# Closing branch A's softmax sums: reciprocals spread by TensorE transposes, or through DRAM by DMA

## The chip, the cores and the metric

The kernel runs on one core of one Trainium2 chip. The metric is the device time of one execution in microseconds. An execution is timed several times; a separate profiled execution leaves a trace, in which the span is the time from its first to its last instruction. The engines are TensorE (PE; its weight loads are PEld), VectorE (DVE), ScalarE (ACT), GpSimd (POOL) and SyncE (SP), which here issues most DMAs. Each engine works its own instruction list strictly from top to bottom, and an instruction that waits holds up all behind it.

## The reference

An encoder layer over two sequences, one of 1024 positions and one of 256 (together T = 1280, ten tiles of 128). Cut to what matters here:

```python
o_a, _ = _banded_attention(qa, ka, va, A_WINDOW, 1, rel_bias[:, :A_HEADS], sink)   # 8 heads of 64
    # inside: denom = sum(p) + exp(sink - m);  o = (p @ v) / denom
o_b = _dilated_mixture(qb, kb, vb, rel_bias[:, A_HEADS:])
merged = gates[:, :, 0] * (o_a.reshape(b, S, A_Q) @ w_branch_a) + gates[:, :, 1] * (o_b @ w_branch_b)
x = x + merged @ w_out
```

The gates are sigmoids of 2 x 1024 columns of the input projection plus a bias. After this come an RMS norm, a squared-ReLU MLP and a last RMS norm. All is float32; a product of two float32 matrices is made of three matmuls on parts that are split into a high and a low half (`hi`, `lo`): ScalarE writes the high half, VectorE subtracts it from the source to get the low half.

## The kernel before, in words

The kernel projects everything first, then runs branch B's attention, then branch A's (eight heads in four units of two, ten tiles of 128 queries each), then the gated merge, then the MLP. The change lies at the seam between branch A's attention and the gated merge, some 665 to 760 us into the span.

**Branch A's attention.** For each pair of tiles, scores are made, exponentiated (ScalarE, which also sums each row into `l_a`, a tile of 128 queries x 8 heads x 10 tiles), turned by TensorE, and multiplied with the values. The result leaves unnormalized to DRAM (`scr_o`, lines 1212 and 1213), already transposed: 128 rows are two heads' 64 channels, columns are queries. `sums_a` (line 1215) closes the sums: it adds the sink's term and takes the reciprocal, in the layout queries x (head, tile). In between TensorE works off `logits` (line 1223), the gates' last projections, whose PSUM blocks ScalarE copies out (`gs`, line 1234) for SyncE to store in DRAM (`scr_g`, line 1235).

**Reciprocals meet the output.** The output has channels on its partitions and the reciprocals have queries there. So `widen` (line 1394) lets GpSimd repeat each reciprocal 64 times (line 1398), and `turn_a` (line 1400) lets TensorE transpose that by four 128x128 transposes per tile into PSUM (line 1408) before VectorE multiplies (line 1409) the reloaded output `o` (`load_o`, line 1387). ScalarE then writes the high half (line 1415) and VectorE the low half (`low_a`, line 1419).

**The gated merge.** `jobs` lists the products: for each of three blocks of columns (512, 512, 256) eight products of branch B, then four of branch A; last, four more of branch A for each block. Below they are numbered from 0: jobs 0 to 7 are branch B's of the first block (six matmuls each), jobs 8 to 11 branch A's of the first block (twelve each). Each product fills one of three PSUM banks named `mm`, which go round: job 7 takes the bank of job 4, and so on. VectorE multiplies the bank with the job's gate (`mT`, line 1535, or `sg`, line 1537), which frees it. Job *i*'s gate is loaded by SyncE (`load_gate`, line 1481: `sg<-scr_g`, 256 KB) six jobs ahead, and ScalarE applies the sigmoid (`open_gate`, line 1486) three jobs ahead. Weights of branch A (`w_a`) are loaded by `fetch` (line 222), and split by `prepare` (lines 231 and 235, `whi` and `wlo`); `weight(0)` at a job calls for the next.

**What sets the order.** Up to `last.close()` the instructions of each engine stand as the code is written. From there, the jobs' loop included, a scheduler places each engine's instructions by its own costs, keeping the order of data. All DMAs named here are on SyncE's one queue. They use eight semaphores in turn, so a DMA also waits for the eighth before it to have landed.

## Time and profile before

| | |
|---|---|
| device time, median of 3 runs | 1674.3 us (1673.67 to 1675.32) |
| span of the profiled execution | 1672.7 us (its device time is not given apart; the median lies 1.6 us above this span) |
| TensorE busy | 1661.8 us (99%), granted clock 1.000 on the mean |
| VectorE, ScalarE, GpSimd busy | 951.1, 714.3, 494.3 us |
| TensorE idle from 655 to 800 us | 0.8 us, one wait, at 695.3 us |

In rows of the trace the number ahead is the start in us from the span's start, the next the duration; "128x512 f32" is partitions by elements of what is written; a bracket at the end holds the idle time of the engine before the row and what ended it. "SPq" rows are DMAs as SyncE issues them, not the transfer itself.

### The profile page before, as it was taken

Reading aid. Unit: us, or ns where it says so; the run is one execution under the profiler, and the core shown is the slowest. Engines: PE = TensorE matmul, PEld = TensorE weight load, DVE = VectorE, ACT = ScalarE, POOL = GpSimd, SP = SyncE. Lnnn points to the kernel's source line nnn. Section 1 sums busy time; section 2 is a strip of 40 time slices with the busy share of each in tenths; the row PEclk is TensorE's granted clock in tenths of the full one; section 3 lists DMA queues with packets and bytes.
Section 4 is the critical chain, followed back from the end, with each engine's and each line's share of the span. In section 5 each row is a group of like instructions: output and inputs, shape, how many; then the busy total and the mean of one; then the engine's idle time right before and its main releaser. Section 6 shows DMA issues by size and latency. Waiting matters only on the chain.

```text
span 1672.7 us, 24767 instructions
## 1 busy us (share of the span) xinstructions
PE 1661.8 (99%) x9256; PEld 1413.9 (85%) x9256; DVE 951.1 (57%) x1534; ACT 714.3 (43%) x1473; POOL 494.3 (30%) x372
## 2 busy tenths in 40 slices
PE   9999999999999999999999999999999999999998
PEld 7898888888888888888888888888888888888886
DVE  6732233455654565667278545445456775867665
ACT  6232323345654655654176333333334333333435
POOL 1212222111112352100100656455554250514240
PEclk9999999999999999999999999999999999999999
DMA  7416552666667794845121443343356934733333
GB/s 256 150 54 126 134 132 75 165 196 189 198 184 228 192 236 134 284 135 193 38 89 59 161 160 120 121 161 125 116 191 230 362 113 137 253 104 107 120 120 126
DMA packets 224176, 262.45 MB, mean 157 GB/s; under 512 B 29486, under 2 KB 153694, under 8 KB 224056
## 3 DMA queue, kind: packets, MB, share of 16 engines
q1 hardware_dynamic: 217000, 242.69, 45.4%
q0 software_dynamic: 6720, 17.65, 5.1%
q8 instruction: 73, 1.20, 0.3%
q10 hardware_dynamic: 336, 0.53, 0.1%
q14 instruction: 47, 0.39, 0.1%
HBM read 175.13 MB, written 90.92 MB: 159 GB/s over the span
## 4 chain that ended last, share of the span: by engine, by line
PE 96%; ACT 2%; DVE 1%; DMA 1%; issue 0%; SPq 0%; DVEq 0%; ACTq 0%
PE dn L345 22%; PE x L345 19%; PE mm L192 14%; PE z L345 10%; PE v L819 6%; PE y L345 5%; PE mm L345 5%; PE pv L345 3%; PE sc L345 3%; PE pt L1193 2%; PE pv L1209 2%; PE sc L553 1%; PE pv L600 1%; PE pt L586 1%; PE tr L336 1%; PE sc L1167 1%
## 5 line engine op out<-in xcount | busy, mean ns | idle before, releaser
L345 PE MATMUL dn<-dhi,ulo 128*128 128x512 f32 x448 | 174.3, 389 | 0.0
L345 PE MATMUL dn<-dlo,uhi 128*128 128x512 f32 x448 | 174.3, 389 | 0.0
L345 PE MATMUL dn<-dhi,uhi 128*128 128x512 f32 x448 | 174.3, 389 | 0.0
L345 PE MATMUL x<-chi,wlo 128*128 128x512 f32 x424 | 166.5, 393 | 0.0
L345 PE MATMUL x<-clo,whi 128*128 128x512 f32 x424 | 165.6, 390 | 0.0
L345 PE MATMUL x<-chi,whi 128*128 128x512 f32 x424 | 165.0, 389 | 0.0
L312 DVE TENSOR_TENSOR wlo<-ta,whi 128x1024 fp32r<-128x1024 f32 x30 | 56.3, 1876 | 174.0 <-ACT whi L310 174.0
L312 DVE TENSOR_TENSOR wlo<-raw,whi 128x1024 fp32r<-128x1024 f32 x60 | 89.6, 1494 | 103.1 <-ACT whi L310 98.2
L391 POOL TENSOR_TENSOR tb<-raw 128x512 f32<-128x512 f32 x25 | 32.3, 1290 | 363.7 <-DMA raw<-in_w_in_dram 111.8
L345 PEld LDWEIGHTS dn<-dhi,ulo 128*128 128x128 f32 x448 | 84.1, 188 | 17.6
L345 PEld LDWEIGHTS dn<-dhi,uhi 128*128 128x128 f32 x448 | 84.1, 188 | 17.4
L345 PEld LDWEIGHTS dn<-dlo,uhi 128*128 128x128 f32 x448 | 84.1, 188 | 17.4
L345 PEld LDWEIGHTS x<-chi,whi 128*128 128x128 f32 x424 | 79.6, 188 | 17.1
L345 PEld LDWEIGHTS x<-chi,wlo 128*128 128x128 f32 x424 | 79.8, 188 | 15.1
L345 PEld LDWEIGHTS x<-clo,whi 128*128 128x128 f32 x424 | 79.8, 188 | 14.6
L1735 POOL TENSOR_TENSOR t<-raw,t 128x1024 f32<-128x1024 f32 x16 | 46.4, 2924 | 149.2 <-DMA raw<-in_w_down_dram 149.2
L186 DVE TENSOR_TENSOR ulo<-uraw,uhi 128x1024 fp32r<-128x1024 f32 x56 | 86.1, 1558 | 4.4 <-ACT uhi L185 4.4
L1886 DVE TENSOR_TENSOR v<-v,dn 128x512 f32<-128x512 f32 x90 | 59.7, 683 | 42.3 <-PE dn L345 42.3
L186 DVE TENSOR_TENSOR dlo<-raw,dhi 128x1024 fp32r<-128x1024 f32 x32 | 50.1, 1590 | 46.3 <-ACT dhi L185 45.3
L1986 POOL TENSOR_TENSOR u<-u,u 128x640 f32<-128x640 f32 x16 | 25.1, 1569 | 173.3 <-ACT u L1904 173.3
L345 PE MATMUL dn<-dhi,up 128*128 128x512 f32 x224 | 73.5, 389 | 0.0
L345 PE MATMUL z<-chi,wlo 128*128 128x512 f32 x184 | 71.6, 389 | 0.0
(319 smaller groups left out, 4619.2 us busy)
## 6 DMA issues: line engine op xcount, KB each, us to landing
scr_u<-u SPq DMA_DIRECT2D x112, 320.0 KB, 2.6
uraw<-scr_u SPq DMA_DIRECT2D x56, 512.0 KB, 3.9
raw<-in_w_down_dram SPq DMA_DIRECT2D x36, 512.0 KB, 6.7
raw<-in_w_up_dram SPq DMA_DIRECT2D x32, 512.0 KB, 5.2
raw<-in_w_in_dram SPq DMA_DIRECT2D x25, 512.0 KB, 5.2
sg<-scr_g SPq DMA_DIRECT2D x32, 256.0 KB, 6.2
uraw<-scr_u SPq DMA_DIRECT2D x28, 256.0 KB, 4.5
qk<-scr_kb SPq DMA_DIRECT2D x48, 128.0 KB, 2.6
```

Source lines behind the costliest of these rows:

```text
L186: nc.vector.tensor_tensor(lo, src, hi.bitcast(F32), op=ALU.subtract)
L192: nc.tensor.matmul(ps, a, b, start=i == 0, stop=i == len(seq) - 1)
L312: nc.vector.tensor_tensor(lo, src, hi.bitcast(F32), op=ALU.subtract)
L336: nc.tensor.transpose(ps[:, P * i : P * (i + 1)], xn[t][:, P * k : P * (k + 1)], ident)
L345: nc.tensor.matmul(ps, a, b, start=first and i == 0, stop=last and i == len(seq) - 1, skip_group_check=True)
L391: (nc.vector if vector else nc.gpsimd).tensor_tensor(o, x, y, op=ALU.subtract)
L819: nc.tensor.matmul(ps[:, :n], a, b, start=k == 0 and j == 0, stop=k == KC - 1 and j == 2)
L1193: nc.tensor.transpose(ps[:, P * k : P * k + P], s[:, h, P * b : P * b + P], ident)
L1209: nc.tensor.matmul(pv[HALVES[h], P * i : P * i + P], src, pt[:, at + 2 * b + h, :], start=b == 0, stop=b == W // P - 1, skip_group_check=True)
L1735: nc.gpsimd.tensor_tensor(o, a, b, op=ALU.subtract)
L1886: nc.vector.tensor_tensor(v, v, ps, op=ALU.add)
L1986: nc.gpsimd.tensor_tensor(u[S1], u21, u22, op=ALU.add)
```

## The change

The repeat on GpSimd, the forty transposes and their PSUM banks go. `sums_a` runs earlier, in the last round of the attention loop, behind the last transposes of scores. A new `rows_a` transposes the reciprocals once (128 x 80 to 80 x 128), VectorE copies them out of PSUM, and SyncE stores these 80 rows (40 KB) in a DRAM buffer `scr_l1`. `widen` now is two DMAs on SyncE for each pair of tiles, each reading four rows' stretches of 256 floats once for each of 64 partitions (256 KB each); `turn_a` multiplies with that tile. Two weights of `w_a` are fetched and split at jobs one lower (0, 3, 4, 7 in place of 1, 4, 5, 8).

```diff
--- before.py
+++ after.py
@@ -277,6 +277,7 @@
     scr_n = dram.tile([2, ROWS * P], F32, name="scr_n")
     scr_c = dram.tile([1, ROWS * P], F32, name="scr_c")
     scr_o = [dram.tile([P, 4, 2, P], F32, name=f"scr_o{t}") for t in range(0, NT, 2)]
+    scr_l1 = dram.tile([AH, T], F32, name="scr_l1")
     scr_x = [dram.tile([P, D], F32, name=f"scr_x{t}") for t in range(NT)]
 
     scr_u = [dram.tile([P, 7, 4, TH], F32, name=f"scr_u{g}") for g in range(FF // P // 8)]
@@ -1212,14 +1213,6 @@
             nc.vector.tensor_copy(o, pv[:, : 2 * P].rearrange("p (i q) -> p i q", i=2))
             nc.sync.dma_start(scr_o[t // 2][:, u], o)
 
-        def sums_a():
-
-            sinks = nsink.unsqueeze(2).to_broadcast([P, AH, NT])
-            nc.vector.tensor_tensor(nm_a, nm_a, sinks, op=ALU.subtract)
-            nc.scalar.activation(nm_a, nm_a, AF.Exp)
-            nc.vector.tensor_tensor(l_a, l_a, nm_a, op=ALU.add)
-            nc.vector.reciprocal(l_a, l_a)
-
         def logits():
 
             for i, c in enumerate(PLAIN):
@@ -1389,24 +1382,12 @@
                 rows_o[t] = slot("o", (P, 4, 2, P))
                 nc.sync.dma_start(rows_o[t], scr_o[t // 2])
 
-        wide_l = {}
-
-        def widen(t):
-
-            r = wide_l[t // 2] = slot("wl", (P, 2, AH, HD))
-            for i in range(2):
-                nc.gpsimd.tensor_copy(r[:, i], l_a[:, :, t + i].unsqueeze(2).to_broadcast([P, AH, HD]))
-
         def turn_a(t):
             if t in (0, 4, 8):
                 o_hi.block(t // 4)
                 o_lo.block(t // 4)
             o = rows_o[t - t % 2][:, :, t % 2, :]
-            ps = bank("pt")
-            r = wide_l[t // 2][:, t % 2].rearrange("p h d -> p (h d)")
-            for k in range(4):
-                nc.tensor.transpose(ps[:, P * k : P * k + P], r[:, P * k : P * k + P], ident)
-            nc.vector.tensor_tensor(o, o, ps.rearrange("p (k q) -> p k q", k=4), op=ALU.mult)
+            nc.vector.tensor_tensor(o, o, wide_l[t // 2][:, :, P * (t % 2) : P * (t % 2) + P], op=ALU.mult)
             per = o_hi.per(P * t)
             parts = [(o_hi.at(k, P * t, P, per), o_lo.at(k, P * t, P, per), o[:, k : k + per, :])
                      for k in range(0, 4, per)]
@@ -1417,6 +1398,32 @@
         def low_a(t):
             for hi, lo, src in banks_t.pop(("a", t)):
                 nc.vector.tensor_tensor(lo, src, hi.bitcast(F32), op=ALU.subtract)
+
+        def sums_a():
+
+            sinks = nsink.unsqueeze(2).to_broadcast([P, AH, NT])
+            nc.vector.tensor_tensor(nm_a, nm_a, sinks, op=ALU.subtract)
+            nc.scalar.activation(nm_a, nm_a, AF.Exp)
+            nc.vector.tensor_tensor(l_a, l_a, nm_a, op=ALU.add)
+            nc.vector.reciprocal(l_a, l_a)
+
+        def rows_a():
+
+            ps, n = bank("mm", "tn"), AH * NT
+            nc.tensor.transpose(ps[:n, :P], l_a.rearrange("p h t -> p (h t)"), ident)
+            rows = a3("o", (P, 2, P), 3)[:n, 0, :]
+            nc.vector.tensor_copy(rows, ps[:n, :P])
+            a = scr_l1[:, :]
+            nc.sync.dma_start(bass.AP(a.tensor, a.offset, [[P, n], [1, P]]), rows)
+
+        wide_l = {}
+
+        def widen(t):
+
+            r = wide_l[t // 2] = slot("wl", (P, 4, 2 * P))
+            a = scr_l1[:, :]
+            for h in range(2):
+                nc.sync.dma_start(r[HALVES[h]], bass.AP(a.tensor, a.offset + T * h + P * t, [[0, HD], [2 * T, 4], [1, 2 * P]]))
 
         load_h21()
         load_prompt(0, unit0[0])
@@ -1444,6 +1451,7 @@
                 for h in range(2):
                     exponential(*order[j + 1], h)
             else:
+                sums_a()
                 steps_of(fill, 2)
                 next(merges, None)
             if j == n - 4:
@@ -1459,9 +1467,11 @@
                 load_o(1)
         prepare()
         values_of(*order[n - 2])
-        sums_a()
         run(merges)
         next(fill)
+        rows_a()
+        widen(0)
+        widen(2)
         prepare()
         w_bs = [weight(0), weight(0)]
         w_as = [None] * 4
@@ -1492,8 +1502,6 @@
         load_gate(3)
         load_o(3)
         for i in range(4):
-            if i < 2:
-                widen(2 * i)
             if i < 3:
                 open_gate(i)
             next(fill)
@@ -1516,10 +1524,10 @@
             for f, t in side.get(i, ()):
                 f(t)
             open_gate(i + 3)
-            if i in (1, 4, 22, 26):
+            if i in (0, 3, 22, 26):
                 fetch()
-            elif i in (5, 8, 33, 35):
-                w_as[(5, 8, 33, 35).index(i)] = weight(0)
+            elif i in (4, 7, 33, 35):
+                w_as[(4, 7, 33, 35).index(i)] = weight(0)
             elif i in (38, 40, 42, 44):
                 prepare()
             hi, lo = w_bs[c // 4] if x == "b" else w_as[c // 2]
```

How the instructions stand, before and in the change, at three places.

SyncE, at the seam (`scr_o` is the attention's output, `scr_g` the gates; `sg_7111` and `sg_7123` are the gates of jobs 0 and 1, `sg_7116` and `sg_7128` those of jobs 2 and 3), before:

```order
L1213 DMA scr_o8_92<-o_7096 128x256
L1481 DMA sg_7111<-scr_g8_134 128x512
L1481 DMA sg_7111<-scr_g9_135 128x512
L1390 DMA o_7114<-scr_o2_89 128x1024
L1481 DMA sg_7116<-scr_g10_136 128x512
L1481 DMA sg_7116<-scr_g11_137 128x512
L1235 DMA scr_g15_141<-gs_7131 128x512
L1235 DMA scr_g15_141<-gs_7160 128x256
L222 DMA raw_7236<-in_w_branch_a_dram 128x4x256
L1235 DMA scr_g15_141<-gs_7188 128x512
```

and in the change:

```order
L1214 DMA scr_o8_92<-o_7101 128x256
L1417 DMA scr_l1_93<-o_7110 80x128
L1426 DMA wl_7113<-scr_l1_93 64x4x256 x2
L1426 DMA wl_7116<-scr_l1_93 64x4x256 x2
L1491 DMA sg_7123<-scr_g8_135 128x512
L1491 DMA sg_7123<-scr_g9_136 128x512
L1383 DMA o_7126<-scr_o2_89 128x1024
L1491 DMA sg_7128<-scr_g10_137 128x512
L1491 DMA sg_7128<-scr_g11_138 128x512
L1228 DMA scr_g15_142<-gs_7137 128x512
L222 DMA raw_7213<-in_w_branch_a_dram 128x4x256
L1228 DMA scr_g15_142<-gs_7166 128x256
```

Five DMAs (the store of the sums and four loads that wait for it) now stand ahead of the first gates, and the first load of `w_a` stands one store earlier.

ScalarE, around the split of the first `w_a` weight (`whi_7309` before, `whi_7283` in the change; `sg_7195` and `sg_7201` are the gates of jobs 6 and 7, `sg_7246` and `sg_7242` those of jobs 8 and 9), before:

```order
L1415 ACTIVATE ohi_0_1_7200<-o_7114 128x2x128
L1486 ACTIVATE sg_7195<-sg_7195,bg_76 128x512
L1486 ACTIVATE sg_7246<-sg_7246,bg_76 128x512
L1415 ACTIVATE ohi_0_0_7199<-o_7114 128x2x128
L1415 ACTIVATE ohi_0_1_7200<-o_7114 128x2x128
L231 ACTIVATE whi_7309<-raw_7236 128x1024
L1486 ACTIVATE sg_7246<-sg_7246,bg_76 128x512
```

and in the change:

```order
L1396 ACTIVATE ohi_0_0_7205<-o_7126 128x2x128
L1396 ACTIVATE ohi_0_1_7206<-o_7126 128x2x128
L1496 ACTIVATE sg_7201<-sg_7201,bg_76 128x512
L1496 ACTIVATE sg_7242<-sg_7242,bg_76 128x512 x2
L231 ACTIVATE whi_7283<-raw_7213 128x1024
L1373 ACTIVATE obhi_1_0_7309<-merged_6282 128x1024
L1496 ACTIVATE sg_7275<-sg_7275,bg_76 128x512
```

The split stood behind job 8's gate and now stands behind job 9's too.

VectorE, around the low half of the same weight (`wlo_7310` before, `wlo_7284` in the change; `mT` rows are jobs' products, in order: `mm_7313`, `mm_7327`, `mm_7338` are jobs 5, 6 and 7 before; `mm_7267`, `mm_7287`, `mm_7299` are jobs 3, 4 and 5 in the change), before:

```order
L1535 TENSOR_TENSOR mT_0_2_7221<-mm_7297,sg_7191 128x512
L1419 TENSOR_TENSOR olo_0_0_7201<-o_7114,ohi_0_0_7199 128x2x128
L1419 TENSOR_TENSOR olo_0_1_7202<-o_7114,ohi_0_1_7200 128x2x128
L1535 TENSOR_TENSOR mT_0_2_7221<-mm_7313,sg_7191 128x512
L235 TENSOR_TENSOR wlo_7310<-raw_7236,whi_7309 128x1024
L1535 TENSOR_TENSOR mT_0_3_7222<-mm_7327,sg_7195 128x512
L1535 TENSOR_TENSOR mT_0_3_7222<-mm_7338,sg_7195 128x512
```

and in the change:

```order
L1543 TENSOR_TENSOR mT_0_1_7223<-mm_7267,sg_7128 128x512
L1400 TENSOR_TENSOR olo_0_1_7208<-o_7126,ohi_0_1_7206 128x2x128
L1400 TENSOR_TENSOR olo_0_0_7207<-o_7126,ohi_0_0_7205 128x2x128
L1400 TENSOR_TENSOR olo_0_1_7208<-o_7126,ohi_0_1_7206 128x2x128
L235 TENSOR_TENSOR wlo_7284<-raw_7213,whi_7283 128x1024
L1543 TENSOR_TENSOR mT_0_2_7224<-mm_7287,sg_7197 128x512
L1543 TENSOR_TENSOR mT_0_2_7224<-mm_7299,sg_7197 128x512
```

The low half stood behind the products of jobs 0 to 5 and now stands ahead of job 4's.

## The prediction

> **What bounds the kernel now.** I read the page first (engines' shares, chain of waits by engine), then TensorE's waits, the chain in order of time at the seam, and the stages around it.
>
> ```profile
> span 1672.7 us, 24767 instructions
> PE 1661.8 (99%) x9256; PEld 1413.9 (85%) x9256; DVE 951.1 (57%) x1534; ACT 714.3 (43%) x1473; POOL 494.3 (30%) x372
> PE 96%; ACT 2%; DVE 1%; DMA 1%; issue 0%; SPq 0%; DVEq 0%; ACTq 0%
> ```
>
> TensorE sets the time: what it does less comes off the span, unless it then waits. So two questions count: what the transposes take of TensorE, and whether the new route makes it wait. The chain from 680 us on, and TensorE's wait there, show how near it is to waiting already:
>
> ```profile
> 680.85 0.44 PE pt L1408 x4
> ...
> 685.04 5.88 DMA sg<-scr_g
> ...
> 690.95 1.39 ACT sg L1486 x2
> 692.33 0.61 ACT ohi L1415 x2
> 692.95 0.96 ACT whi L231
> ...
> 694.03 1.20 DVE wlo L235
> ...
> 695.27 4.84 PE mm L192 x20
> ```
>
> ```profile
> PE mm L192 <- DVE wlo L235: 0.8, 1, 0.8
> ```
>
> At 695.27 job 8, branch A's first product, starts 0.8 us late. It waits for `w_a`'s low half; that for the high half on ScalarE, which stands behind the gates of jobs 7 and 8; and job 7's gate, issued at 685.04, takes 5.88 us to land. Those loads are slow because the DMA engines are full:
>
> ```profile
> 674.00:682.00 8.00, 8.00 (x44) 6.85 (x43) 0.68 (x1) 4.04 (x7) 3.94 (x8) 1.00 0.60 196
> 682.00:690.00 8.00, 8.00 (x44) 6.66 (x43) 5.66 (x13) 4.12 (x9) 0.15 (x1) 1.00 0.99 306
> 690.00:700.00 10.00, 9.20 (x44) 7.45 (x43) 8.80 (x14) 8.61 (x14) 2.20 (x2) 1.00 1.04 385
> ```
>
> The last columns are granted clock, DMA share, GB/s. From 682 us this stretch is bound by DMA as much as by TensorE; only up to 682 is there a hole.
>
> **What goes.** The forty transposes.
>
> ```profile
> L1408 PE MATMUL pt<-ident,wl x40: 270/272/277, 680.7 to 724.4; 128*128 128x128 f32 x40
> ```
>
> ```profile
> 685.71 1.03 PE L1408 MATMUL pt<-ident,wl 128*128 128x128 f32 x8
> 686.50 0.48 PE L192 MATMUL mm<-obhi,wlo 128*128 128x512 f32 x1
> 686.81 0.40 PE L192 MATMUL mm<-oblo,whi 128*128 128x512 f32 x1
> ```
>
> One lasts 272 ns, but they overlap. Eight take 685.71 to 686.50, and the matmul behind them gives way 0.31 us later where its kind does so 0.23 us later: 0.79 + 0.08 = 0.87 us, 0.109 each. Forty are 4.4 us, less 0.1 for the one new transpose of 80 rows: **-4.3 us**, of which 24 (2.6 us) lie ahead of job 8 and 16 (1.75 us) behind. GpSimd's ten repeats held up nothing but these. VectorE's ten multiplies stay at one length, with SBUF in place of PSUM.
>
> **What the seam now waits for.** VectorE's rows there, and SyncE's:
>
> ```profile
> 667.70 0.69 DVE L272 COPY pt<-pt 128x512 f32<-128x512 f32 x1 [0.66 <-PE pt L1193]
> 670.51 0.42 DVE L1212 COPY o<-pv 128x256 f32<-128x256 f32 x1 [0.46 <-PE pv L1209]
> 670.85 0.23 DVE L1218 TENSOR_TENSOR nm_a<-nm_a,nsink 128x80 f32<-128x80 f32 x1
> 671.76 0.65 DVE L1221 RECIPROCAL l_a<-l_a 128x80 f32<-128x80 f32 x1
> 672.43 1.23 DVE L235 TENSOR_TENSOR wlo<-raw,whi 128x1024 fp32r<-128x1024 f32 x1
> ```
>
> ```profile
> 671.34 0.91 SPq L1481 DMA_DIRECT2D sg<-scr_g  x2
> 672.82 0.85 SPq L1481 DMA_DIRECT2D sg<-scr_g  x2
> 681.94 2.58 SPq L1481 DMA_DIRECT2D sg<-scr_g  x3
> ```
>
> ```profile
> scr_o<-o SPq DMA_DIRECT2D x2, 128.0 KB, 1.9
> sg<-scr_g SPq DMA_DIRECT2D x4, 256.0 KB, 3.2
> sg<-scr_g SPq DMA_DIRECT2D x8, 256.0 KB, 6.8
> ```
>
> ```profile
> L1333 SPq DMA_DIRECT2D r<-scr_c x36: 450/605/2234, 579.3 to 639.0; - x36
> ```
>
> The sums take 670.85 to 672.41, 1.56 us. Behind the copy that ends at 668.39 they end at 670.0. A low half (1.23), the last output's copy (0.42) and the copy of the 80 rows (no row; nothing to 0.42, I take 0.3) follow: 672.0. The store lands 1.9 us after issue (the nearest store, 670 us): 674.0. Only then SyncE issues the four broadcast loads. The nearest are branch B's broadcast coefficients (L1333): 0.6 us each to issue, so 676.4. The first gates, of jobs 0 and 1, go out at 676.5 and 677.0 in place of 671.34 and 671.8, the pair behind them at 677.9 in place of 672.82: **all 5.1 us later**.
>
> Who waits for gates: ScalarE, and behind it the copies that free TensorE's banks.
>
> ```profile
> 674.16 1.56 ACT L1486 ACTIVATE sg<-sg,bg 128x512 f32<-128x512 f32 x2 [0.46 <-DMA sg<-scr_g]
> 675.63 0.58 ACT L1234 ACTIVATE gs<-mm 128x512 f32<-128x512 f32 x1
> 679.43 0.72 ACT L1486 ACTIVATE sg<-sg,bg 128x512 f32<-128x512 f32 x1 [3.22 <-DMA sg<-scr_g]
> 680.06 0.36 ACT L1234 ACTIVATE gs<-mm 128x256 f32<-128x256 f32 x1
> 680.94 0.60 ACT L1234 ACTIVATE gs<-mm 128x512 f32<-128x512 f32 x1
> ```
>
> Jobs 0, 1 and 2 take the banks of the last three logits blocks, which these three `gs` rows free. Job 1's gate lands 3.2 us after issue at the earliest, 680.2, and at 6.8 us latest, 683.8; 1 MB of broadcasts (3.4 us at 306 GB/s, from 675.5) ahead of it lets me take 680.5. Then its sigmoid (0.72) and `gs` (0.58): job 0 starts at 681.8 in place of 680.8, a stall of 1.0 us (0.7 to 4.3). Job 2's gate took 679.43 - 672.82 = 6.6 us from issue to sigmoid, an output load of 512 KB ahead of it as now: 684.5 (681.1 at 3.2 us). Sigmoid, second `gs` (0.36), third (0.60): 686.2.
>
> SyncE has the stores of these blocks ahead of job 4's gate, so that goes out at **686.5 in place of 681.94, 4.5 us later** (at the light end 683.1, 1.2 later). From here the queue holds the same loads as before, at full DMA: gates 4, 5, 6, output, 7, 8, output, 9. One helps: `w_a`'s 512 KB now goes out ahead of the second store and has moved by then, 1.3 us at 385 GB/s. Job 9's gate had landed when ScalarE came to it:
>
> ```profile
> 686.50 1.54 SPq L1481 DMA_DIRECT2D sg<-scr_g  x2
> 693.80 1.32 ACT L1486 ACTIVATE sg<-sg,bg 128x512 f32<-128x512 f32 x2
> ```
>
> Issued at 686.50, it landed 6.8 us later at 693.3 (no wait at 693.80 agrees). Now: 693.3 + 4.5 - 1.3 = 696.5.
>
> **Where it ends on the path.** The order puts the high half of `w_a` behind job 9's gate, and the low half ahead of job 4's product on VectorE. So the earlier split brings a new wait: job 7 needs job 4's bank, whose product waits for the low half, which waits for a gate used two jobs later. From 696.5: sigmoid 0.66, high half 0.96, low half 1.20, product 0.68, gaps 0.2: job 7 starts at 700.2. It has six matmuls, 1.37 us: job 8 starts at 701.6 in place of 695.27, **+6.3 us**, in which the 24 transposes ahead of it and the old 0.8 us wait are already contained. Behind it 1.75 us of transposes are saved. The remaining `wl` loads (512 KB per pair, 1.3 us of DMA) meet gates that are six jobs ahead, and branch A's products last 2.7 us; I take nothing. **Sum: +6.3 - 1.75 = +4.6 us**, span 1677.3. The median lies 1.6 us above the profiled span: **1678.9 us**. Ends: with light loads job 4's gate goes out at 683.1, job 9's lands at 693.2, job 8 starts at 698.3: +1.3, 1675.6. With job 1's gate at its late end, 683.8, job 2's lands 2.5 us behind (768 KB at 306 GB/s), 686.3 and 1.8 later than taken: +6.4, 1680.7.
>
> **Rivals.**
>
> *The loads slip into the hole.* At 674 to 682 us the DMA share is 0.60. If broadcasts and gates all land in there, job 9's gate at 692.0, job 8 starts at 697.1: +1.8 - 1.75, 1674.3, no change. For it: the hole; a gate landed in 3.2 us there. Against: SyncE can't use the hole before the store has landed at 674.0, and over 2 MB (four broadcasts, three gates, one output) go ahead of the second store. [...]
>
> *All is hidden, the transposes' price comes off.* TensorE never waits: -4.3 and the old 0.8: 1669.2. Job 8 would start at 695.27 - 0.8 - 2.6 + 0.1 = 692.0, job 7 at 690.6, and for that job 9's gate would have to land by 686.9, 6.4 us before it did without the extra 1 MB. The order itself speaks against it.
>
> *The stall also costs clock.* From the second `gs` (685.6) jobs 1 to 6 last 8.2 us, to 693.8 or, with waits for banks, some 2 us more; so job 7's start at 700.2 leaves TensorE 4 to 6 us without a matmul. What such a gap does, the trace shows at its end alone (the column ahead of the last two is the clock):
>
> ```profile
> 1665.43 0.39 PE L345 MATMUL dn<-dhi,up 128*128 128x512 f32 x1
> 1671.00:1672.70 1.70, 0.00 (x0) 0.00 (x0) 0.00 (x0) 0.00 (x0) 0.00 (x0) 0.52 0.00 0
> ```
>
> The last matmul ends at 1665.82; from 1671 on, 5.2 us later, half a clock is granted. If the gap is long enough, and half clock lasts as long as the gap, 5 us, 2.5 us are lost: 1681.4. [...]
>
> **How the numbers follow.** The forecast has a chance of 0.51 (own range 1675.6 to 1680.7), the lost clock 0.24, the hole 0.19, all hidden 0.06. Within 0.2% (3.3 us, about what a measurement of this kernel tells from no change) means up to 1677.6: all of the hole case and, as job 9's gate may land 1.3 us earlier than summed, about a sixth of the forecast (0.09). So faster 0.06, same 0.28, slower 0.66. The range, 1675.0 to 1683.0, covers both ends of the sum and the clock case, and leaves out the hidden case and about half of the hole.
>
> **What would show it.** Right: no `pt` transposes at jobs; the first gate issued near 676.5; TensorE waiting at job 0 for `gs` (about 1 us) and at job 7 for VectorE, this the longest (4 to 6 us); `whi` of the first `w_a` weight behind a gate that ScalarE waited for; job 8 near 701.6. Wrong, if job 7 starts without a wait, if the store or the broadcasts land much sooner than 1.9 us and 3 us, or if stalls turn up outside 675 to 705 us. The clock case shows as a granted clock below 1.00 behind job 7.

## The result, and the profile after

The changed kernel takes **1683.4 us** (median of 5 runs, 1682.55 to 1684.23); the kernel before took 1675.3 us beside it (5 runs, 1673.67 to 1675.64). The ratio is 1.0047 with a 95% interval of 1.0036 to 1.0058: slower by 8.2 us. The forecast was 1678.9 us, with a range that ended at 1683.0, 0.4 us short of the measured time. The direction and the place were right; 4.5 us were missing from the sum.

The page of the changed kernel, with its span, its engines and its chain of waits by engine:

```profile
span 1681.6 us, 24675 instructions
...
PE 1664.1 (99%) x9217; PEld 1414.2 (84%) x9217; DVE 952.5 (57%) x1535; ACT 714.5 (42%) x1473; POOL 487.0 (29%) x362
...
PE 95%; ACT 1%; DMA 1%; DVE 1%; SPq 0%; issue 0%; ACTq 0%
```

There are 39 matmuls fewer, and yet TensorE is busy 2.3 us longer. TensorE's waits (line waited for: us in total, times, longest) say where to look:

```profile
PE mm L192 <- DVE mT L1543: 5.3, 2, 4.9
PE mm L192 <- ACT gs L1227: 3.3, 1, 3.3
```

Both lie at the seam. The chain in order of time from the sums to job 0 (start, us, what):

```profile
672.13 0.30 DVE o L1415
...
672.45 1.48 DMA scr_l<-o
...
673.94 0.58 SPq L1426
...
676.60 6.08 DMA sg<-scr_g
...
682.70 1.38 ACT sg L1496 x2
684.08 0.49 ACT gs L1227
...
684.62 9.52 PE mm L192 x30
```

The store of the rows lands at 673.92, four broadcast loads are issued, and only then the first gate, at 676.60. That gate takes 6.08 us, so that job 0 starts at 684.62 in place of 681.04. (The chain goes on with the load of `w_a`'s second weight, which landed at 702.70. Job 7 needs nothing of it, and the product that job 7 waits for had begun at 702.00; so the rows below are followed instead.) Then SyncE's rows for jobs 4 to 9, and what ScalarE and VectorE wait for ahead of job 7:

```profile
687.18 2.92 SPq L1491 DMA_DIRECT2D sg<-scr_g  x3
...
690.63 0.90 SPq L1491 DMA_DIRECT2D sg<-scr_g  x2
...
692.06 0.60 SPq L1491 DMA_DIRECT2D sg<-scr_g  x1
```

```profile
695.64 1.39 ACT L1496 ACTIVATE sg<-sg,bg 128x512 f32<-128x512 f32 x2 [0.47 <-DMA sg<-scr_g]
699.16 0.72 ACT L1496 ACTIVATE sg<-sg,bg 128x512 f32<-128x512 f32 x1 [2.13 <-DMA sg<-scr_g]
699.79 1.04 ACT L231 ACTIVATE whi<-raw 128x1024 fp32r<-128x1024 f32 x1
```

```profile
700.86 1.23 DVE L235 TENSOR_TENSOR wlo<-raw,whi 128x1024 fp32r<-128x1024 f32 x1 [4.56 <-ACT whi L231]
702.00 1.88 DVE L1543 TENSOR_TENSOR mT<-mm,sg 128x512 f32<-128x512 f32 x3
```

The row at 699.16 is job 9's gate, issued at 692.06 and waited for; `w_a`'s high half stands behind it, VectorE's low half behind that, and behind the low half the product of job 4, whose bank job 7 needs. Job 7 starts at 702.74 after 4.93 us of idle TensorE, and job 8 behind its six matmuls:

```profile
702.74 0.79 PE L192 MATMUL mm<-obhi,wlo 128*128 128x512 f32 x1 [4.93 <-DVE mT L1543]
...
705.47 0.63 PE L192 MATMUL mm<-ohi,wlo 128*128 128x512 f32 x1
```

Last, the stretches; the column ahead of the last two is TensorE's granted clock:

```profile
674.00:682.00 8.00, 7.36 (x40) 6.05 (x39) 1.29 (x2) 0.00 (x0) 0.00 (x0) 1.00 0.84 203
682.00:690.00 8.00, 5.38 (x13) 4.22 (x14) 2.65 (x5) 5.17 (x11) 0.00 (x0) 0.59 0.90 296
690.00:700.00 10.00, 7.42 (x31) 5.42 (x29) 3.98 (x9) 5.47 (x11) 0.00 (x0) 0.99 1.00 303
700.00:710.00 10.00, 7.26 (x22) 5.80 (x23) 7.83 (x10) 7.57 (x13) 0.00 (x0) 0.66 1.08 315
710.00:725.00 15.00, 15.00 (x68) 12.40 (x67) 12.36 (x24) 8.19 (x17) 0.00 (x0) 1.00 1.05 297
```

Two things to see. In each of the two stalls the clock falls to half (0.59 and 0.66 on the mean of the stretch; the clock records have half clock from 683.43 and from 700.50 on, 6.83 us each time), so job 7's six matmuls last 2.73 us in place of 1.37 and job 8 starts at **705.47 in place of 695.27**. And the DMA engines, which had spare time from 710 us on before the change (share 0.35 from 710 to 725), are now full to 725 (1.05): ten broadcast loads of 256 KB have come in.

### The profile page after: what moved, and what is told of

It reads as the page before. It is cut to its first block, busy times and chain, and to the rows that moved or that the text cites. A ratio compares the mean times of both kernels' runs of the same rounds, so it can differ in the third digit from the quotient of the medians.

```text
span 1681.6 us, 24675 instructions
## 1 busy us (share of the span) xinstructions
PE 1664.1 (99%) x9217; PEld 1414.2 (84%) x9217; DVE 952.5 (57%) x1535; ACT 714.5 (42%) x1473; POOL 487.0 (29%) x362
## 4 chain that ended last, share of the span: by engine, by line
PE 95%; ACT 1%; DMA 1%; DVE 1%; SPq 0%; issue 0%; ACTq 0%
PE dn L346 22%; PE x L346 19%; PE mm L192 14%; PE z L346 10%; PE v L820 6%; PE y L346 5%; PE mm L346 5%; PE sc L346 3%; PE pv L346 3%; PE pt L1194 2%; PE pv L1210 2%; PE sc L554 1%; PE pv L601 1%; PE pt L587 1%; PE tr L337 1%; PE sc L1168 1%
```

## The experiments

The times are medians; the kernel before, run beside each, lay at 1674.9 to 1675.3. The trace of a kernel is of one of the executions timed. All kernels are changes of the changed kernel (1683.4; run once more beside others, 1683.7) or of the kernel before. Four causes were set against each other: **queue** (store and broadcasts stand ahead of the first gates on SyncE), **bandwidth** (the broadcasts' bytes), **order** (the split of `w_a`, and what it stands behind), **clock**.

### Where the loads stand on the queue

The store and all broadcasts on GpSimd's queue in place of SyncE's:

```diff
-            nc.sync.dma_start(bass.AP(a.tensor, a.offset, [[P, n], [1, P]]), rows)
+            nc.gpsimd.dma_start(bass.AP(a.tensor, a.offset, [[P, n], [1, P]]), rows)
-                nc.sync.dma_start(r[HALVES[h]], ...)
+                nc.gpsimd.dma_start(r[HALVES[h]], ...)
```

> The store of the sums' rows and the ten pairs of broadcast loads are issued by GpSimd in place of SyncE; nothing else differs from the changed kernel (1683.4 us). Queue theory (the store and the four broadcasts stand ahead of the first gates on SyncE and make all gates 5 us late): the gates of jobs 0 and 1 are issued near 671.5, as in the kernel before, and land at 674 to 675; job 0 starts near 681 with no wait over 0.5 us, job 8 by 695, no half clock, and the time is 1672 to 1676 us. Bandwidth theory (the 1 MB of broadcasts takes the DMA engines' time wherever it is issued): the gates go out early, but job 2's gate and those behind it still land 4 us or more later than before; TensorE still waits 3 us or more at job 0 or job 7, 1679 to 1683 us. Order theory (the split of w_a a product sooner, by itself, makes job 7 wait): the wait at job 7 stays, smaller than 4.9 us, 1677 to 1680 us.

Measured: 1683.3 us, ratio 1.0052 (1.0038 to 1.0065); no gain. TensorE doesn't wait at job 0 any more, but the waits only move:

```profile
PE mm L192 <- DVE mT L1543: 7.1, 2, 4.9
```

The gates of jobs 0 to 3 went out early, as expected; what stood behind them took longer (a 256 KB gate issued from 668 to 706 us took 9.1 us from issue to landing on the median, 7.3 in the changed kernel). The queue isn't all that differs here: GpSimd issued the last three pairs' loads 11 to 18 us sooner than SyncE does (the third by 680.3 in place of 692.79), and on ScalarE the high half came to stand behind job 8's gate. Nor did it help to leave all on SyncE and let the first gates go ahead:

```diff
+        def store_rows():
+            nc.sync.dma_start(bass.AP(a.tensor, a.offset, [[P, AH * NT], [1, P]]), sums_rows[0])
-        widen(0)
-        widen(2)
         (gates of jobs 0 to 3, output load)
+        store_rows()
+        widen(0)
+        widen(2)
```

> The changed kernel (1683.4 us) with the store of the sums' rows and the first two pairs of broadcast loads moved on SyncE behind the gates of jobs 0 to 3 and the output load between them; the bytes stay the same. Queue theory: these gates are issued by 674.5 in place of 676.6 and later and land by 678, TensorE doesn't wait at job 0, and job 7 starts 4 to 5 us sooner than at 702.7, the half clock goes with the wait: 1675 to 1678 us. Bandwidth theory (1 MB of broadcasts delays whatever is issued behind it): the wait at job 0 goes, but the gates and w_a behind the broadcasts land no sooner than before, job 7 or 8 waits longer in exchange, 1681 to 1684 us.

Measured: 1685.7 us, ratio 1.0058 (1.0044 to 1.0072), longer than either theory had it. Its trace is of the longest of the five executions (1690.4 us), of which some 5 us went far ahead of the seam, in 10.24 us of half clock from 11.75 us on. At the seam job 0 doesn't wait, and two later waits take 10.0 us:

```profile
PE mm L192 <- DVE mT L1549: 10.0, 2, 5.3
```

The queue theory falls twice: whose turn came first on the queue changed where TensorE waited, and didn't shorten the time (1683.3 and 1685.7 us).

### Are the broadcasts slow because 64 partitions read the same rows?

```diff
-                nc.sync.dma_start(r[HALVES[h]], bass.AP(a.tensor, ...))
+                if (t, h) == (0, 0): (as before)
+                else:
+                    rows = x_sample[0, 256 * (t // 2 % 4) : ..., 512 * h : 512 * h + 256]
+                    nc.sync.dma_start(r[HALVES[h]], rows.rearrange("(k p) n -> p k n", p=HD))
```

> The changed kernel, with all broadcast loads but the first reading as many bytes, in packets of the same 1 KB, from rows of the input x that differ for each partition, in place of the same few rows of the sums for 64 partitions; so all but the first half tile leave the true reciprocals out. Shared-row theory (1 KB packets took 74 ns on the mean in these loads and 52 ns in those of w_a because 64 partitions read the same rows): the packets take about 52 ns, the 1 MB lands 1.0 to 1.5 us sooner, jobs 0 and 7 start as much sooner, 1681.5 to 1682.5 us. Plain bandwidth theory (they are slow because four loads lie in the engines at once): packets stay near 74 ns, 1683 to 1684 us.

Measured: 1682.5 us, ratio 1.0047 (1.0034 to 1.0059). The 1024 packets of the first four loads took 72 ns on the mean against 74, a load 9.0 us from issue to landing on the median against 7.4. A second trace of the changed kernel itself has 81 ns and 8.9 us, so that these differences are no more than two executions of one kernel show. The shared rows cost nothing that can be seen here.

### How many bytes

Every broadcast cut to one head of four, in the place they have and with the first gates ahead:

```diff
-            r = wide_l[t // 2] = slot("wl", (P, 4, 2 * P))
+            r = wide_l[t // 2] = slot("wl", (P, 1, 2 * P))
-                 [[0, HD], [2 * T, 4], [1, 2 * P]]
+                 [[0, HD], [2 * T, 1], [1, 2 * P]]
```

> The changed kernel with each broadcast load cut to one head in place of four: as many loads, in the same place, behind the same store, with a quarter of the packets (128 KB for a pair in place of 512); the multiplies use that head's reciprocals for all four, so the true ones of three heads are left out. Bandwidth theory: of the 1 MB ahead of the first gates 0.75 MB goes, 2.5 us at 306 GB/s to 3.5 us at 4.7 us for the MB, and 0.4 MB more of the third pair ahead of job 9's gate, 1.3 us; job 7 starts 4 to 5 us sooner, near 698, its wait falls to 1 us or less, no half clock ahead of job 8: 1674.5 to 1677.5 us. Queue theory (issue behind the store and four loads is what counts, not the bytes): the first gates are still issued at 676.6, job 7 starts no more than 1.5 us sooner, 1681 to 1683 us.

> Both at once: the store and the first two pairs of broadcast loads behind the first four gates, and each load cut to one head (the reciprocals of the other three are left out). Queue and bandwidth theories alike: neither position nor bytes are left, TensorE waits at job 0 and job 7 for less than 1 us in all, and what remains is the forty transposes saved: 1670 to 1673 us. Order theory (w_a split a product sooner is a cause by itself): job 7 still waits 2 us or more for VectorE's low half, 1674 to 1677 us. If e1 alone and the quarter loads alone each gain half of it, the two add; if one of them alone reaches this time, that one is the cause.

Measured: 1677.6 us and 1677.8 us (ratios 1.0015 and 1.0017). Each lies somewhat above the time expected of it. The cut gains 5.8 us, the queue's order nothing on top of it. To tell the 1 MB ahead of the first gates from the 1.5 MB behind, each was cut alone (`n = 1 if t < 4 else 4`, and the opposite), with the changed kernel run once more beside them:

> The changed kernel with only the first two pairs of broadcast loads cut to one head of four (their other reciprocals are left out): 0.75 MB less ahead of the first gates, while the last three pairs come in full. If the 1 MB ahead of the first gates is what costs (the term that the forecast took at 3.4 us), nearly all of the 5.8 us that cutting all five pairs gained comes back: 1677.5 to 1679 us. If the later pairs, which the forecast priced at nothing, cost as well: 1680 to 1682 us.

> The opposite: the first two pairs of broadcast loads in full, the last three cut to one head of four (their other reciprocals are left out). If only the 1 MB ahead of the first gates costs: no change, 1682.5 to 1684 us, with both long waits as in the changed kernel. If the later pairs cost as well: 1679.5 to 1681.5 us.

> The changed kernel itself, as the measure for the others of these runs: 1682.5 to 1684.5 us by all theories, with waits of 3 us or more at job 0 and of 4 to 5.5 us at job 7, and half clock behind each.

Measured: 1683.6, 1678.3 and 1683.7 us. This was a surprise, the first two outside all that was expected: cutting the 1 MB for which the forecast had a price gains nothing on the median, and cutting the 1.5 MB that it took at nothing gains 5.4 us. (The first of these traces is of the shortest of five executions, 1681.3 us; there job 8 starts 2.2 us sooner, at 703.25.) But the traces show that more than bytes had changed. ScalarE with the first two pairs cut, and with the last three cut:

```profile
693.19 1.39 ACT L1498 ACTIVATE sg<-sg,bg 128x512 f32<-128x512 f32 x2
696.94 0.72 ACT L1498 ACTIVATE sg<-sg,bg 128x512 f32<-128x512 f32 x1 [2.36 <-DMA sg<-scr_g]
697.57 1.04 ACT L231 ACTIVATE whi<-raw 128x1024 fp32r<-128x1024 f32 x1
```

```profile
695.96 1.40 ACT L1498 ACTIVATE sg<-sg,bg 128x512 f32<-128x512 f32 x2 [0.85 <-DMA sg<-scr_g]
697.26 1.04 ACT L231 ACTIVATE whi<-raw 128x1024 fp32r<-128x1024 f32 x1
699.25 0.72 ACT L1498 ACTIVATE sg<-sg,bg 128x512 f32<-128x512 f32 x1 [0.95 <-DMA sg<-scr_g]
```

In the second the high half stands ahead of job 9's gate. The scheduler, which orders each engine by its own costs, had answered smaller loads with another order. So in all three runs that gained, bytes and order were mixed.

### The order, with the bytes in full

ScalarE's order for jobs 0 to 7 written by hand, the high half behind job 8's gate; then the same with the split back at the products of the kernel before:

```diff
+        hand.enter_context(tc.manual_schedule(engines={mybir.EngineType.Activation}))
         for i, (x, b, c) in enumerate(jobs):
+            if i == 8:
+                hand.close()
+            if i == 0:
+                open_gate(3)
...
-            open_gate(i + 3)
+            if i:
+                open_gate(i + 3)
+            if i == 5:
+                w_as[0] = weight(0)
```

> The changed kernel with all its loads in full, and one thing moved: on ScalarE the high half of the first w_a weight (and the high half of branch B's next block) stands behind job 8's gate in place of job 9's, as it came to stand by itself in the kernels with the later broadcasts cut (1677.6 and 1678.3 us); ScalarE's order is written out by hand for jobs 0 to 7, the other engines' order stays, but for one multiply on VectorE behind job 7. Order theory (that gate, used two jobs later, is what the cut loads took off the path): the high half starts 2.5 us sooner, near 697.2, job 7 near 700.2, 1677.5 to 1680.5 us. Bandwidth theory (the later 1.5 MB itself costs the 5.5 us): job 8's gate lands late as well, job 7 no sooner than 702, 1682 to 1684 us.

> As the run with the split back where the kernel before has it (1682.9 us; there the high half still stood behind job 9's gate), and ScalarE's order written out so that it stands behind job 8's, as in the kernel before; all loads in full. If order is all that the later loads' cut changed: the low half is ready 2.5 us sooner, job 8 starts near 701.5 in place of 704.3, 1678.5 to 1681 us. If the bytes count by themselves: job 8 near 704, 1682 to 1684 us.

Measured: 1681.5 us (1679.45 to 1682.6) and 1681.6 us (1680.43 to 1684.25). In the first ScalarE now reads:

```profile
695.86 1.40 ACT L1496 ACTIVATE sg<-sg,bg 128x512 f32<-128x512 f32 x2 [1.02 <-DMA sg<-scr_g]
697.16 1.04 ACT L231 ACTIVATE whi<-raw 128x1024 fp32r<-128x1024 f32 x1
700.30 0.72 ACT L1496 ACTIVATE sg<-sg,bg 128x512 f32<-128x512 f32 x1 [1.15 <-DMA sg<-scr_g]
```

The high half starts 2.6 us sooner, job 7 at 700.11, job 8 at 702.79. Job 9's gate isn't any sooner. So one place on ScalarE's list is worth 2 us of the 8. Against the run with the last three pairs cut, which has the split at the same place (1678.3), 3.2 us more go with the later broadcasts' bytes. These two traces don't show where: the one of the cut kernel is of the longest of its eleven executions (1681.6 us), and has job 8 at 702.94, no sooner.

The second run shows one way in which these loads cost. ScalarE comes to the high half another 1.7 us sooner, yet VectorE starts the low half at 700.96 only:

```profile
695.49 1.05 ACT L231 ACTIVATE whi<-raw 128x1024 fp32r<-128x1024 f32 x1
```

```profile
700.35 0.69 DVE L1390 TENSOR_TENSOR o<-o,wl 128x512 f32<-128x512 f32 x1 [3.89 <-DMA wl<-scr_l]
700.96 1.22 DVE L235 TENSOR_TENSOR wlo<-raw,whi 128x1024 fp32r<-128x1024 f32 x1
```

With the split back, the multiply of the third pair of tiles stands ahead of the low half, and it waits for its broadcast, whose two loads were issued from 690.96 on, 9.4 us ahead of the multiply. Job 8, at 702.23, waits for that load and no longer for a gate. In the changed kernel this multiply stands behind the low half (703.80).

### The split of `w_a` sooner, by itself

In the kernel before, with its transposes, and in the kernel before without transposes:

```diff
-            if i in (1, 4, 22, 26):
+            if i in (0, 3, 22, 26):
-            elif i in (5, 8, 33, 35):
-                w_as[(5, 8, 33, 35).index(i)] = weight(0)
+            elif i in (4, 7, 33, 35):
+                w_as[(4, 7, 33, 35).index(i)] = weight(0)
```

> The kernel before (1675.2 us) with one part of the change alone: the load and the split of the first two w_a weights a product sooner; transposes and GpSimd's repeats stay. Order theory (the split sooner is a cause by itself): VectorE's low half stands ahead of the product of job 3 or 4 and job 7 waits for it; 1676.5 to 1678.5 us. Rival (at the loads of the kernel before, the gates ahead of the high half land in time, and job 8 starts as soon or up to 0.8 us sooner): 1674.4 to 1675.5 us.

> The kernel before without the forty transposes (GpSimd's widened sums multiplied in as they stand, so the turning is left out; 1672.7 us) and with the split of w_a a product sooner: the changed kernel's savings and its order of the split, without any store or broadcast. Order theory: job 7 waits for the low half, 1674 to 1676 us. Rival: without the new loads the gates land in time and nothing waits longer, 1672 to 1673.2 us.

Measured: 1678.5 us, ratio 1.0021 (1.0012 to 1.0030), and 1675.3 us against 1672.7 without it: **2.6 to 3.4 us lost by that part alone**. In the first, VectorE's low half is ready no sooner (694.22; 693.99 in the kernel before), but it now stands behind four products in place of six: those of jobs 4 and 5 have to wait for it, and so has job 7, with half clock behind the wait. (The bracket names GpSimd's copy; the high half, which the low half needs, ended at the same time, 694.13.)

```profile
694.22 1.51 DVE L235 TENSOR_TENSOR wlo<-raw,whi 128x1024 fp32r<-128x1024 f32 x1 [2.93 <-POOL wl L1398]
695.66 0.68 DVE L1535 TENSOR_TENSOR mT<-mm,sg 128x512 f32<-128x512 f32 x1
```

```profile
696.39 0.80 PE L192 MATMUL mm<-obhi,wlo 128*128 128x512 f32 x1 [3.06 <-DVE mT L1535]
```

Taking the split back in the changed kernel, in full and with gates first and a quarter of the bytes (the diff is the one above, reversed):

> The changed kernel, with the load and the split of w_a back at the products where the kernel before has them; the sums, the store and the broadcasts stay on SyncE. Order theory (the low half of the first w_a weight stands ahead of job 4's product on VectorE, so that job 7 waits for a gate used two jobs later): the low half moves behind the products of jobs 4 and 5; the wait of 4.9 us at job 7 goes or becomes a smaller one (1 to 3 us) at job 7 or 8, job 8 starts near 702 in place of 705.5, and the time is 1679.5 to 1681.5 us. Queue theory alone (only the gates' lateness counts): the wait moves to job 8, which starts no sooner than 704.5; 1682.5 to 1684 us. In both the wait of 3.3 us at job 0 stays as it is.

> Gates first and a quarter of the broadcast bytes, as in the run that had both (1677.7 us; the reciprocals of three heads of four are left out), and the split of w_a back where the kernel before has it. Order theory (what kept that run 5 us above the kernel without transposes is VectorE's order, with the low half ahead of job 4's product): the waits at jobs 5 and 7 go down to 1.6 us, the half clock goes, 1672.5 to 1674.5 us. Rival (what is left is the 0.25 MB of loads and the store, and VectorE's low halves of o ahead of the products of jobs 1 and 2, which the split doesn't touch): job 5 still waits 2.9 us and half clock still follows, 1676.5 to 1678 us.

Measured: 1682.9 and 1678.8 us; nothing is gained. In the first the low half stands behind job 4's and job 5's products, and job 8 waits for it directly:

```profile
PE mm L192 <- DVE wlo L235: 6.0, 1, 6.0
```

The high half still waits there for job 9's gate and ends at 701.20; the low half starts at 703.07, since ahead of it stands, as above, the multiply of the third pair (702.46), which waited for its broadcast. In the second run the wait of 2.7 us at job 5 stays, ahead of which the split doesn't stand, and the high half came to stand behind job 9's gate, where without the edit it stood behind job 8's. So neither run moves the split alone, and what the sooner split costs in the changed kernel they don't tell. In the kernel before, where the gates are in time, it is what makes the wait.

### The clock

Matmuls that nobody reads, ahead of jobs 0 and 7, to keep TensorE at work:

```diff
+        last.enter_context(tc.manual_schedule(engines={mybir.EngineType.PE}))
+            if i in (0, 7):
+                idle = bank("pt")
+                for r in range(12 if i == 0 else 18):
+                    nc.tensor.matmul(idle, hi[:, r % 2, cols], src[0].at(r % 2, t0, n), start=True, stop=True)
```

> The changed kernel, with matmuls that nobody reads put on TensorE ahead of job 0 (12) and ahead of job 7 (18), in a bank of their own, so that TensorE is not idle while it waits. They are extra work, and no computation is left out. Clock theory (each of the two idle stretches, 3.3 and 4.9 us, costs 6.8 us of half clock, the second one on the path): the granted clock stays at 1.00 from 683 to 708, job 7 takes 1.4 in place of 2.7 us, and the time falls by 1.5 to 2.5 us, to 1681 to 1682. Rival (half clock costs nothing, since the products behind it are bound by DMA and by the copies anyway): 1683 to 1684 us.

Measured: 1681.5 us (four runs from 1680.71 to 1681.86, one of 1687.81, which makes the ratio's interval, 1.0032 to 1.0059, no narrower than the changed kernel's). The trace is clearer than the time:

```profile
682.00:690.00 8.00, 7.81 (x34) 5.83 (x33) 4.01 (x8) 5.20 (x11) 0.00 (x0) 1.00 0.91 300
690.00:700.00 10.00, 7.74 (x28) 5.94 (x27) 2.63 (x6) 6.16 (x11) 0.00 (x0) 0.83 1.02 303
700.00:710.00 10.00, 10.00 (x45) 8.15 (x44) 9.07 (x12) 7.18 (x13) 0.00 (x0) 1.00 1.08 314
```

Behind both fillers the clock stays at 1.00 (0.59 and 0.66 without them). It drops once, for 3.41 us, behind a gap of 2.26 us at another job that had no filler. Job 8 starts at 703.66, 1.8 us sooner. Half clock costs about 2 us of the 8. The changed kernel's own trace agrees: job 7 takes 1.36 us longer than at full clock, and half clock lasts until 707.33, 1.86 us into job 8, which loses 0.93, together 2.3 us.

### What the transposes were worth

```diff
-            ps = bank("pt")
-            for k in range(4):
-                nc.tensor.transpose(ps[:, P * k : P * k + P], r[:, P * k : P * k + P], ident)
-            nc.vector.tensor_tensor(o, o, ps.rearrange("p (k q) -> p k q", k=4), op=ALU.mult)
+            nc.vector.tensor_tensor(o, o, r.rearrange("p (k q) -> p k q", k=4), op=ALU.mult)
```

> The kernel before without the forty transposes: GpSimd's widened sums are multiplied in as they stand, so the turning of the reciprocals is left out; nothing else differs. Term of the forecast: 40 x 0.109 = 4.4 us less, 1670.4 us (1669.5 to 1671.5). Rival (DMA sets the start of job 8 at 695.27 already, so that only the 16 transposes behind it count): job 8 still starts near 695, with a longer wait, 1.7 to 2 us less: 1672.8 to 1673.3 us.

Measured: 1672.7 us, ratio 0.9988 (0.9978 to 0.9998). The rival holds. TensorE gets to the seam's jobs sooner and waits instead, 1.6 us at job 5, and job 8 starts where it did:

```profile
690.20 0.50 PE L192 MATMUL mm<-obhi,wlo 128*128 128x512 f32 x1 [1.62 <-DVE mT L1532]
...
695.09 0.50 PE L192 MATMUL mm<-ohi,wlo 128*128 128x512 f32 x1 [0.52 <-DVE wlo L235]
```

Ahead of job 8 the transposes lay in time that TensorE would have spent waiting for loads; only the sixteen behind it were to be had.

### A version that is faster than both

That gives a mixture: the kernel before, with its sums and its split where they were and its first 24 transposes; the reciprocals are turned once at job 8, and only the last two pairs of tiles take theirs from broadcasts, near jobs 9 and 13.

```diff
 def widen(t):
+            if t >= 6: (two broadcast loads from scr_l1, as in the change)
 def turn_a(t):
+            if t >= 6: (multiply with the loaded tile)
-                6: [(high_b, 1)], 7: [(low_b, 1)],
+                6: [(high_b, 1)], 7: [(low_b, 1)], 8: [(rows_a, 0)],
```

> A mixture that computes everything: the kernel before with its sums, gates, split and the first 24 transposes as they were; only the reciprocals of the last two pairs of tiles, whose 16 transposes stand behind job 8, are turned once (at job 8), stored, and come back as broadcasts of 0.5 MB each near jobs 9 and 13. Bandwidth theory: by then the DMA engines have spare time (share 0.35 from 710 us in the kernel before) and nothing waits for these loads; 16 x 0.109 less one new transpose, 1.6 us less: 1673 to 1674.2 us. Rival (1 MB more at 697 to 712 us, still full there, delays the gates of jobs 14 on): TensorE waits at a job behind 14, 1675 to 1678 us.

Measured: **1672.3 us** (11 runs, 1671.61 to 1673.95), ratio 0.9983 (0.9973 to 0.9992): 2.9 us faster than the kernel before, 11 faster than the changed one. TensorE has no wait of over 0.2 us at the seam, and job 8 starts at 694.58. Of the gain of 2.4 us between the two profiled spans, 1.7 lie behind job 8, the price of the sixteen transposes; the rest comes with the 0.8 us wait at job 8, which this execution doesn't have. The broadcasts go out at 699.5 and 703.4; with them the DMA engines are busy from 710 us on, too (share 0.93 in place of 0.35), and the clock stays up:

```profile
690.00:700.00 10.00, 9.89 (x46) 8.00 (x45) 9.33 (x15) 9.11 (x15) 0.00 (x0) 1.00 0.96 342
700.00:710.00 10.00, 10.00 (x48) 8.28 (x47) 8.30 (x17) 4.95 (x12) 0.00 (x0) 1.00 1.06 297
710.00:725.00 15.00, 15.00 (x68) 12.43 (x67) 10.93 (x19) 8.83 (x18) 0.00 (x0) 1.00 0.93 289
```

The third pair, too, from a broadcast (`t >= 4`, the reciprocals turned at job 6, its load at job 7):

> As the mixture of transposes and broadcasts (1672.3 us), but with the third pair of tiles by broadcast too: the reciprocals are turned at job 6, and 0.5 MB comes back near job 7, while the DMA engines are still full. It saves eight transposes more, 0.9 us. Bandwidth theory: 0.5 MB at 300 to 340 GB/s is 1.5 to 1.7 us of DMA time taken from gates and w_a's second load, so that TensorE waits at jobs 9 to 12: 1673 to 1676 us. Rival (behind job 7 the gates have a lead of six jobs): 1671.2 to 1672.2 us.

Measured: 1675.7 us, ratio 1.0004 (0.9993 to 1.0014): all of the gain is gone again. A wait is back ahead of job 8, and half clock behind it, together some 3.3 us in the trace:

```profile
696.23 0.80 PE L192 MATMUL mm<-ohi,wlo 128*128 128x512 f32 x1 [2.44 <-DVE wlo L235]
```

```profile
698.99 1.52 SPq L1402 DMA_DIRECT2D wl<-scr_l  x2
```

But the third pair's load can't have made this wait: it was issued at 698.99, and the reciprocals stored at 696.40, both behind job 8's start. The chain ahead of job 8 goes back to job 7's gate, issued at 684.91, which took 6.96 us to land, 5.01 in the mixture; up to there the two kernels issue the same loads. So the loss is measured, and that the 0.5 MB cause it is not shown.

## Why the forecast was right in its place and short in its sum

The runs make a ladder from the kernel before to the changed one. Each step is a difference of two medians, by their spread good to about 1 us, and holds for the kernel at which it was taken:

| step | from, to | us |
|---|---|---|
| transposes away | 1675.2, 1672.7 | -2.5 |
| split a product sooner | 1672.7, 1675.3 | +2.6 |
| store, a quarter of the broadcasts and earlier sums, GpSimd's repeats away | 1675.3, 1677.6 | +2.3 |
| first two pairs in full | 1677.6, 1678.3 | +0.7 |
| last three pairs in full, the split at the same place on ScalarE | 1678.3, 1681.5 | +3.2 |
| high half one gate later on ScalarE | 1681.5, 1683.4 | +1.9 |

Half clock, some 2 us, is contained in these steps.

The traces say where the loss lies. Take the span behind job 8's start, less TensorE's waits there and half of the time at half clock. Without the last sixteen transposes this rest is 975.2 to 975.7 us in seventeen traces of these kernels and 976.1 in one; with them it is 977.4 and 977.3. The changed kernel has 975.23, and 975.20 with a quarter of the broadcasts. So what the changed kernel lost in its trace, it lost ahead of job 8, or by half clock behind it.

- *The transposes, -4.3 us, of which 1.75 behind job 8.* VectorE's ten multiplies did stay at one length (679 ns before, 684 in the change, on the median). As a price for TensorE it was too much, 2.5 measured; but the sum took only the 1.75, since it placed job 8 by the loads. Right in the sum, and the run without transposes shows why: job 8 at 695.09. Behind job 8 that run saves 1.9 us, the changed kernel 2.2.
- *Sums to first gate: 672.0, 674.0, issue at 676.5.* 672.43, 673.92 and 676.60. Right.
- *1 MB of broadcasts at 3.4 us, job 0 at 681.8 after 1.0 us.* Mis-sized in the trace: job 0 at 684.62 after 3.26 us, near the late end. But with these two pairs cut, the median stayed where it was.
- *Job 4's gate at 686.5, job 9's landed at 696.5.* 687.18 and 699.16. **This is the step that failed**: job 9's gate was 2.7 us later than summed, and with it job 7 started at 702.74 in place of 700.2, 2.5 us. One of the 2.7 us is later issue (692.06 in place of 691.0); 1.3 were credited for `w_a`'s sooner load, and the trace has no such gain; 0.3 are a landing of 7.1 us in place of 6.8.
- *The order: high half behind job 9's gate, low half ahead of job 4's product, job 7 waiting longest.* Right, row for row in the trace. A run with the split alone gives 2.6 to 3.4 us for it in the kernel before, one with ScalarE's order alone 2 us in the changed kernel.
- *The stall also costs clock, 2.5 us, chance 0.24.* It did, twice, and the second time on the path: 2.3 us in the trace, about 2 by the filler run. **This is the other term that failed**: the sum had it at nothing. The forecast had seen the gap of 4 to 6 us, and priced the loss about right, by an estimate of 5 us at half clock (6.83 in the trace); what it lacked was a row for a short gap. The two terms, 2.5 and 2.3 us, less 0.45 that was saved behind job 8 beyond the 1.75, make 4.35; the profiled span was 4.3 us longer than forecast (1681.6 for 1677.3).
- *Remaining broadcasts: "I take nothing".* Behind job 8, for which the forecast argued, the traces bear it out (975.23 against 975.20). But cutting these loads gains 5.4 us, 3.2 of them with the split at the same place. Of the three pairs only the third is issued early enough to act ahead of job 8, at 692.79, right behind job 9's gate. Where its multiply stands ahead of the low half, in the two runs with the split back, it holds up job 8. In the changed kernel it stands behind; whether its load slowed the gates there, no trace shows.
- *Rivals.* The hole's case is out (a gate landed 6.1 us after issue, not 3.2), and so is the hidden case. Queue position, on which the whole chain of the forecast hung, is not a cause by itself: with the loads elsewhere, the time was the same or longer (1683.3 and 1685.7 us).

What stays open: how the later broadcasts cost 3.2 us in the changed kernel, why `w_a`'s sooner load freed nothing, and what slows the mixture with a third pair by broadcast. Each trace is one execution, and half clock, which lasted 3.41 or 6.83 us at a time at the seam, covers smaller differences.

## What to carry to other kernels

Work on the busiest engine was worth its price only where that engine wasn't about to wait anyway (the forty transposes: 2.5 us measured where 4.4 were expected): ask for each stage whether the next start is set by loads, before counting what is removed. A transfer that trades engine time for DMA time paid where nothing on the path waited behind it, in the mixture (2.9 us): its loads went out behind job 8, with no wait of over 0.2 us to follow. List for it every instruction that stands behind its consumer, too: one multiply that waited 3.89 us for its load held up a split that was ready. And where a scheduler sets the order, a change of a size moves instructions: compare the order of the waiting engine in both kernels before calling a difference bandwidth.

## What the runs showed of the hardware

**Half clock after short gaps.** A gap of 2.40 us was enough, one of 1.62 us wasn't: in the kernel without transposes, whose row is shown above (1.62), the stretch from 690 to 700 us ran at 1.00. With all broadcasts cut to a quarter:

```profile
692.19 0.50 PE L192 MATMUL mm<-obhi,wlo 128*128 128x512 f32 x1 [2.40 <-DVE mT L1543]
```

```profile
690.00:700.00 10.00, 6.15 (x19) 4.58 (x20) 6.13 (x11) 6.90 (x13) 0.00 (x0) 0.83 0.98 334
```

Over the seams of all traces of this case, each of 11 gaps from 3.06 to 6.46 us was met by half clock, 14 of 17 gaps from 2.18 to 2.97 us were, and none of 13 from 0.67 to 1.80 us was; half clock lasted 3.41 or 6.83 us at a time. In the changed kernel's trace it lasted 6.83 us from 683.43 on and 6.83 us from 700.50 on, with 10.24 us of full clock between. A stall at the same place cost more in one execution than in another: the changed kernel's first brought 6.83 us of half clock in one (3.26 us of waiting) and 3.41 in another (2.83). Why some of the 17 gaps were met by half clock and three weren't, no run shows.

**GpSimd's queue made no room.** The same 2.5 MB issued by GpSimd landed no sooner (8.8 us a load on the median, 7.4 on SyncE), and SyncE's gates took 9.1 us in place of 7.3. Six of the ten loads went out 11 to 18 us sooner than on SyncE, so that the queue and the place in line aren't told apart.
